# A fixed engine order for the row norms ahead of three projections, and the setup loads on ScalarE's queue

## The chip, the cores and the metric

The kernel runs on one core of a Trainium2 chip. The metric is the device time of one execution in microseconds (us). The engines are named as in the profile: PE (TensorE, matmuls and transposes), DVE (VectorE), ACT (ScalarE), POOL (GpSimd) and SP (SyncE, which here only issues DMAs). Each engine works through its own instructions in a fixed sequence and waits for the others by semaphores.

## The reference

The kernel computes one layer on 1024 rows of 1024 float32 numbers: a feed-forward half step, two attentions side by side, and a second feed-forward half step, each behind a row norm.

```python
def rms_norm(x, g):
    y = xf * lax.rsqrt(jnp.mean(xf * xf, axis=-1, keepdims=True) + EPS)
    return (y * g.astype(jnp.float32)).astype(x.dtype)

def swiglu_ffn(x, w_in, w_out):
    gate, up = jnp.split(x @ w_in, 2, axis=-1)
    return (jax.nn.silu(gate) * up) @ w_out
...
        x = x + 0.5 * swiglu_ffn(rms_norm(x, ffn1_norm[li]), ffn1_w_in[li], ffn1_w_out[li])
        u = rms_norm(x, mix_norm[li])
        proj = u @ w_mix_in[li]
...
        g_a, g_b = jnp.split(jax.nn.sigmoid(gate_logits + b_gate[li]), 2, axis=-1)
        merged = g_a * (y_a @ w_branch_a[li]) + g_b * (y_b @ w_branch_b[li])
        x = x + merged @ w_o[li]
        x = x + 0.5 * swiglu_ffn(rms_norm(x, ffn2_norm[li]), ffn2_w_in[li], ffn2_w_out[li])
    return rms_norm(x, final_norm)
```

The change touches the three norms ahead of `ffn1_w_in`, `w_mix_in` and `ffn2_w_in`, the first products of these three projections, and the loads of small tables (`lambda_*`, `subln_g`, `b_gate` and the two bias tables).

## The kernel before

**Products.** A projection is done block by block of 1024 x 1024 by 256 columns, called a pair: two column blocks `c1` and `c2` of 128 columns. Each pair is seven products instead of eight (`PRODUCTS`, line 158), in the manner of Strassen and Winograd. The operands of the activations are A11, A12, S1, S2, S3, S4 and A22, where S1 to S4 are sums and differences of the four quadrants; those of the weights are B11, B21, B22 and the differences T1, T2, T3 and N4. One product is twelve matmuls of 128x512: four steps over k, and for each three matmuls (`mm3`, line 126: high by high, high by low, low by high), since every operand is split into a rounded high part and a low rest. `split` (line 94) does that: ACT casts the high part (line 97), DVE subtracts it from the source (line 102). In the rows `whi` and `wlo` are the parts of a weight, `S1h` and `S1l` those of S1, and so on.

**The norm.** Rows 0 to 511 (four tiles of 128 rows, t = 0 to 3) are the first half, rows 512 to 1023 the second. For a tile, ACT squares and sums the row (line 174), DVE adds epsilon, POOL takes the power -1/2 (`r`, line 139), DVE multiplies row, `r` and gain. Then PE transposes the tile (line 208, eight transposes of 128x128), and ACT and DVE make the operands from it. The first half gives A11 and A12 (`norm0`). A tile of the second half gives, with the tile of the first half, S1 and in its place the source of S3 (`norm1a`), then S2 and S4 (`norm1b`), then S3 and A22 split (`norm1c`).

**Begun pairs.** Products 0 (A11 by B11) and 2 (A12 by B21) need the first half alone. So five pairs (`HEADS`, line 49; seven in the mixer) are begun with these two products (`Pair.head`, line 343) while the second half is normed. `Combine` (line 266) keeps the accumulation banks: one product is left in its bank for the chain that goes on in it, the other is copied out by ACT (`c`, line 287) and DVE adds the second product to that copy (`c<-prod,c`, line 113), called the take below. PSUM has six banks of tag "mm" for products and two of tag "tr" for transposes. After the second half is there, `Pair.rest` does the five remaining products of every pair; it loads both weight blocks (512 KB each, `raw`).

**Where it happens.** The norm ahead of the first feed-forward part stands at lines 657 to 689. Those ahead of the mixer and the second feed-forward part are the three callbacks of `renorm` (line 545); `late` (line 564) is their second half and runs when the last outputs of the projection before are out (`xc<-po`, line 522).

**What sets the order.** A scheduler orders the instructions on each engine; the code's order and the buffers limit it. Buffers rotate: ten slots `raw` (rows and weight blocks), ten `w` (split weights), ten `f` (temporaries of 256 KB), three `t` (weight differences). `setup` (line 601) loads the small tables on POOL's queue when the program begins; `le` (line 776) is the exponential of a `lambda` dot product on ACT.

Of the kernel before, what the change touches and what calls it, by code (L numbers as in the profile page):

```python
# [16 lines left out]
P = 128  # L17
# [37 lines left out]
def hybrid_layer_kernel(ctx, tc, x, ffn1_norm, ffn1_w_in, ffn1_w_out, mix_norm, w_mix_in,  # L55
# [165 lines left out]
    def norm1a(t, row0, row1, u, ps):  # L221

        a11, (a21, a22) = by_k(halves(row0.x)[0]), [by_k(h) for h in halves(row1.x)]
        t22 = turned(halves(row1.x)[1], ps)
        nc.scalar.copy(out=a22, in_=t22)
        t21 = turned(halves(row1.x)[0], ps)
        s1 = row1.s1 = temp([P, 4, P], "s1")
        add(s1, t21, a22)
        put(u, "S1", t, s1)
        add(a21, a11, t21, ALU.subtract)  # L230

    def norm1b(t, row0, row1, u):

        a11, a12 = (by_k(h) for h in halves(row0.x))
        add(a11, row1.s1, a11, ALU.subtract)
        put(u, "S2", t, a11)
        add(a12, a12, a11, ALU.subtract)
        put(u, "S4", t, a12)

    def norm1c(t, row1, u):  # L240

        for half, name in zip(halves(row1.x), ("S3", "A22")):
            put(u, name, t, by_k(half))
# [75 lines left out]
    class Pair:  # L319
# [23 lines left out]
        def head(self):  # L343
            r1 = self.load(0)
            get = weight_ops({"B11": r1[:, :4], "B21": r1[:, 4:]}, [P, 4, P])
            for m in (0, 2):
                self.product(m, get)
                self.todo.remove(m)
# [16 lines left out]
    def ffn_in(w_in, u, ps, extra=None):  # L365
# [48 lines left out]
        for p in pairs[:HEADS]:  # L414
            p.head()
            yield
# [128 lines left out]
    def renorm(x_dst, gain, u, ps, projection, extra_heads=0):  # L545
# [12 lines left out]
        def mid(rows):  # L558
            for t in range(4):
                row1.append(Row(rows[t]))  # L560
                nc.sync.dma_start(out=x_dst[4 + t][:, HALF:], in_=rows[t][:, HALF:])
                row1[t].take_right(gain)

        def late(rows):
            u.update(new_u(("S1", "S2", "S4")))
            for t in range(4):
                nc.sync.dma_start(out=x_dst[4 + t][:, :HALF], in_=rows[t][:, :HALF])
                row1[t].take(0)
                row1[t].scale_halves(gain)
                norm1a(t, row0[t], row1[t], u, ps)  # L570
            for _ in range(4 + extra_heads):
                next(projection, None)
            for t in range(4):
                norm1b(t, row0[t], row1[t], u)
            next(projection, None)
            u.update(new_u(("S3", "A22")))
            for t in range(4):
                norm1c(t, row1[t], u)
        return early, mid, late
# [21 lines left out]
    def setup(ps):  # L601
# [7 lines left out]

        for q, k in ((lambda_q1, lambda_k1), (lambda_q2, lambda_k2)):  # L610
            qk = []
            for v in (q, k):
                vt = small.tile([P, B_DIM], F32, tag="lv", bufs=2, name="lv")
                nc.gpsimd.dma_start(out=vt, in_=v[0].partition_broadcast(P))
                qk.append(vt)
            dot = small.tile([P, 1], F32, tag="dot", name="dot")
            nc.vector.tensor_tensor_reduce(out=qk[0], in0=qk[0], in1=qk[1], scale=1.0, scalar=0.0,
                                           op0=ALU.mult, op1=ALU.add, accum_out=dot)
# [19 lines left out]
        yield  # L638
        ea = stage([P, EA], "ea")
        n_clip = EA - (2 * REL_CLIP + 1)  # L640
        nc.gpsimd.dma_start(out=ea[:, n_clip:], in_=spread(rel_bias_a[0], A_HEADS, 2 * REL_CLIP + 1))
# [5 lines left out]
        nc.gpsimd.dma_start(out=tb, in_=spread(t5_bias, B_HEADS, 32))  # L647
# [9 lines left out]
    with tc.tile_pool(name="ps1", bufs=1, space=PSUM) as ps:  # L657

        u = new_u(U_OPS)
        ones = const.tile([1, P], F32, name="ones")  # L660
        nc.vector.memset(ones, 1.0)
        gain = sb.tile([P, D], F32, tag="gain", bufs=1, name="gain")
        for part in range(2):
            g_row = wtemp([1, HALF], "g_row")
            nc.scalar.dma_start(out=g_row, in_=ffn1_norm[0][part * HALF:(part + 1) * HALF].rearrange("(o d) -> o d", o=1))
            pg = ps.tile([P, HALF], F32, tag="mm", bufs=6, name="pg")
            nc.tensor.matmul(pg, ones, g_row, start=True, stop=True)
            nc.scalar.copy(out=halves(gain)[part], in_=pg)
        ffn1 = ffn_in(ffn1_w_in[0], u, ps, setup(ps))
        row0, row1 = [], []  # L670
        for t in range(4):
            row0.append(Row(load(rows(x)[t], raw_tile([P, D], "xt"))))
            row0[t].take()
            row0[t].scale(gain)
            norm0(t, row0[t], u, ps)
        next(ffn1, None)
        for t in range(4):
            row1.append(Row(load(rows(x)[4 + t], raw_tile([P, D], "xt"))))
            row1[t].take()
            row1[t].scale(gain)  # L680
            norm1a(t, row0[t], row1[t], u, ps)
        for _ in range(3):
            next(ffn1, None)
        for t in range(4):
            norm1b(t, row0[t], row1[t], u)
        next(ffn1, None)
        for t in range(4):
            norm1c(t, row1[t], u)
# [60 lines left out]
        def mixer_in():  # L749
# [5 lines left out]
            for p in pairs[8:15]:  # L755
                p.head()
                yield
# [8 lines left out]
        mix = mixer_in()  # L766
        out_projection(ffn1_w_out[0], stored, FFN_ORDER, FFN_LOADS, 0.5, rows(x), x_mid, ps,
                       *renorm(x_mid, gain, u2, ps, mix, 2))
# [237 lines left out]
    with tc.tile_pool(name="ps3", bufs=1, space=PSUM) as ps:  # L1006

        mo = {(th, g): big([P, 4, HALF], f"m{th}{g}", F32) for g in range(2) for th in range(2)}
        for jj in range(KT // 2):
            wr = load(w_cols(w_branch_b[0], jj * 256, 256, 0, 4), raw_tile([P, 4, 256]))  # L1010
            for odd in range(2):
                j = 2 * jj + odd
                w = split_units(wr[:, :, odd * P:(odd + 1) * P], branch_unit)
                for th in range(2):
# [4 lines left out]
                    for k in range(4):  # L1019
# [5 lines left out]
        ffn2 = ffn_in(ffn2_w_in[0], u3, ps)  # L1025
        out_projection(w_o[0], lambda n, i: mo[int(n[1]), i // 4][:, i % 4, :], WO_ORDER, WO_LOADS, 1.0, x_mid, x_mix, ps,
                       *renorm(x_mix, gain, u3, ps, ffn2))
# [59 lines left out]
```

## Time and profile before

| | us |
|---|---|
| median of 3 runs | 2115.09 (2113.3 to 2116.64) |
| the profiled execution | 2114.65 |
| its span in the trace | 2112.9 |
| PE busy | 2045.6 (97% of the span) |
| DVE busy, ACT busy | 1379.1 (65%), 955.5 (45%) |

In rows of the timeline the columns are: start in us, duration in us, engine, line, operation, output<-inputs, shape, count, and in brackets the idle time of the engine just before and what ended it. Rows of windows give the stretch, its length, then busy time and (number of instructions) of PE, the weight load, DVE, ACT and POOL, the granted clock of PE (1.00 is full), the DMA share and GB/s. Durations overlap on one engine: its instructions follow each other somewhat faster than they last.

### The profile page before, as it was taken

What the parts mean: (1) busy time and instruction counts of PE and PEld (TensorE: products, weight loads), DVE (VectorE), ACT (ScalarE), POOL (GpSimd) and SP (SyncE); (2) the same over time, 40 slices, a digit from 0 to 9 for tenths busy, and PEclk for the clock granted to TensorE, in tenths of its full rate; (3) what the DMA queues carried; (4) which work ended last, traced back from release to release, by engine and by line L of the source; (5) the groups of instructions that cost most, each with busy time, mean ns of one, the idle gap of its engine ahead of it and who ended that gap; (6) DMA issues with size and microseconds to landing.
All of it is one profiled execution on the core that took longest, in us unless ns stands there. A gap on an engine that the chain in (4) does not pass through costs nothing.

```text
span 2112.9 us, 28240 instructions
## 1 busy us (share of the span) xinstructions
PE 2045.6 (97%) x9901; PEld 1700.4 (80%) x9901; DVE 1379.1 (65%) x2459; ACT 955.5 (45%) x1825; POOL 142.8 (7%) x202
## 2 busy tenths in 40 slices
PE   6899999999999999999999999999899999999997
PEld 4688888888888788899877888787788888888886
DVE  6765656658567856654657787668766666668566
ACT  6433333334446644433467666157433333334444
POOL 2300000000001000000046211000000000000001
PEclk9999999999999999999999999999999999999999
DMA  5743323376344644743495365644542333275334
GB/s 166 213 135 100 125 86 104 105 261 214 99 135 143 195 135 130 234 145 115 158 302 178 111 221 167 229 139 127 163 144 91 125 96 107 92 278 201 99 116 160
DMA packets 272996, 324.61 MB, mean 154 GB/s; under 512 B 15070, under 2 KB 167662, under 8 KB 272852
## 3 DMA queue, kind: packets, MB, share of 16 engines
q1 hardware_dynamic: 271664, 319.55, 46.2%
q0 software_dynamic: 1184, 3.24, 0.6%
q8 instruction: 78, 1.28, 0.2%
q14 instruction: 66, 0.54, 0.1%
q10 hardware_dynamic: 4, 0.00, 0.0%
HBM read 221.74 MB, written 100.99 MB: 153 GB/s over the span
## 4 chain that ended last, share of the span: by engine, by line
PE 86%; DVE 6%; issue 3%; ACT 2%; DMA 2%; POOL 0%; SPq 0%; ACTq 0%; DVEq 0%; POOLq 0%
PE prod L128 19%; PE prod L129 19%; PE prod L130 18%; PE po L129 7%; PE po L128 7%; PE po L130 7%; PE pt L822 2%; DVE wlo L102 2%; PE pv L906 1%; PE pb L128 1%; PE pb L129 1%; PE pb L130 1%; PE sc L806 1%; PE sc L807 1%; PE pv L970 1%
## 5 line engine op out<-in xcount | busy, mean ns | idle before, releaser
L129 PE MATMUL po<-wlo,whi 128*128 128x512 f32 x744 | 291.1, 391 | 1.9 <-DVE wlo L102 1.8
L130 PE MATMUL po<-whi,wlo 128*128 128x512 f32 x744 | 289.6, 389 | 0.0
L97 ACT CAST whi<-raw 128x512 fp32r<-128x512 f32 x200 | 124.1, 622 | 294.3 <-PE prod L129 224.4
L97 ACT CAST whi<-T 128x512 fp32r<-128x512 f32 x192 | 119.1, 622 | 260.5 <-PE prod L129 248.0
L97 ACT CAST whi<-B 128x512 fp32r<-128x512 f32 x186 | 115.8, 622 | 262.1 <-PE po L129 255.0
L113 DVE TENSOR_TENSOR c<-prod,c 128x512 f32<-128x512 f32 x190 | 130.9, 690 | 146.1 <-PE prod L130 130.0
L102 DVE TENSOR_TENSOR wlo<-B,whi 128x512 fp32r<-128x512 f32 x186 | 128.1, 689 | 139.4 <-ACT whi L97 139.4
L102 DVE TENSOR_TENSOR wlo<-T,whi 128x512 fp32r<-128x512 f32 x192 | 131.8, 688 | 116.0 <-ACT whi L97 104.6
L128 PE MATMUL po<-whi 128*128 128x512 f32 x744 | 201.2, 390 | 0.0
L102 DVE TENSOR_TENSOR wlo<-raw,whi 128x512 fp32r<-128x512 f32 x200 | 137.3, 688 | 92.5 <-ACT whi L97 59.4
L129 PEld LDWEIGHTS po<-wlo,whi 128*128 128x128 f32 x744 | 139.6, 188 | 33.3 <-DVE wlo L102 4.6
L128 PEld LDWEIGHTS po<-whi 128*128 128x128 f32 x744 | 139.4, 188 | 29.0 <-ACT whi L97 0.2
L130 PEld LDWEIGHTS po<-whi,wlo 128*128 128x128 f32 x744 | 139.8, 188 | 28.4
L139 POOL TENSOR_TENSOR r<-v,neg_half 128x1 f32<-128x1 f32 x32 | 29.0, 913 | 1362.9 <-DVE v L180 1288.3
L102 DVE TENSOR_TENSOR wlo<-N,whi 128x512 fp32r<-128x512 f32 x64 | 44.1, 690 | 108.4 <-PE prod L129 69.0
L102 DVE TENSOR_TENSOR wlo<-ha,whi 128x512 fp32r<-128x512 f32 x154 | 105.5, 685 | 9.3 <-ACT whi L97 9.3
L287 ACT COPY c<-prod 128x512 f32<-128x512 f32 x186 | 102.1, 585 | 17.2 <-issue 10.5
L128 PE MATMUL prod<-A11h,whi 128*128 128x512 f32 x240 | 96.4, 402 | 7.9 <-DVE c L113 6.7
L816 ACT ACTIVATE pm<-pm,mn 128x640 f32<-128x640 f32 (+7 forms) x128 | 93.9, 735 | 19.7 <-DVE mn L814 17.0
L97 ACT CAST whi<-ha 128x512 fp32r<-128x512 f32 x154 | 94.8, 615 | 16.9 <-PE prod L129 11.4
L128 PE MATMUL prod<-A12h,whi 128*128 128x512 f32 x240 | 94.7, 394 | 3.4 <-DVE c L113 3.4
L814 DVE CUSTOM_DVE_ANT_0 pm<-sc,nb 128x640 f32<-128x640 f32 (+7 forms) x128 | 87.6, 701 | 14.7 <-PE sc L807 9.8
(236 smaller groups left out, 5018.8 us busy)
## 6 DMA issues: line engine op xcount, KB each, us to landing
raw<-in_ffn_w_in_dram SPq DMA_DIRECT2D x98, 512.0 KB, 4.2
raw<-in_w_mix_in_dram SPq DMA_DIRECT2D x47, 512.0 KB, 4.7
ha<-hS SPq DMA_DIRECT2D x88, 256.0 KB, 2.6
hA<-c SPq DMA_DIRECT2D x66, 256.0 KB, 4.1
ha<-hA SPq DMA_DIRECT2D x66, 256.0 KB, 2.7
B<-in_ffn_w_out_dram SPq DMA_DIRECT2D x12, 1024.0 KB, 11.7
hS<-hs SPq DMA_DIRECT2D x44, 256.0 KB, 2.4
hS<-c SPq DMA_DIRECT2D x44, 256.0 KB, 4.2
```

The lines of the kernel that those rows point to most:

```text
L97: nc.scalar.copy(out=hi, in_=src)
L102: (nc.gpsimd if on_pool else nc.vector).tensor_tensor(out=lo, in0=src, in1=h, op=ALU.subtract)
L113: nc.vector.tensor_tensor(out=out_, in0=a, in1=b, op=op)
L128: nc.tensor.matmul(ps, a[0], b[0], start=first, stop=False, skip_group_check=shared)
L129: nc.tensor.matmul(ps, a[0], b[1], start=False, stop=False, skip_group_check=shared)
L130: nc.tensor.matmul(ps, a[1], b[0], start=False, stop=last, skip_group_check=shared)
L139: nc.gpsimd.tensor_tensor(out=r, in0=v, in1=neg_half, op=ALU.pow)
L287: nc.scalar.copy(out=self.held[name], in_=p)
L806: nc.tensor.matmul(sc[:, m, :wc], qs[:, h, c], ks[:, h, kc], start=True, stop=False)
L814: nc.vector.tensor_tensor_reduce(out=d3, in0=sc, in1=nb.rearrange("p (n w) -> p n w", n=n), scale=1.0, scalar=3e38, op0=ALU.add, op1=ALU.m ...
L816: nc.scalar.activation(out=dst, in_=dst, func=AF.Exp, bias=mn, scale=-1.0, accum_out=rs)
L822: nc.tensor.transpose(pt[:, b, :], p, ident)
```

## The change

The first norm and the second halves in `renorm` are now written in a fixed order for each engine (`in_order`): ACT, DVE and PE in `renorm.late`, and POOL and SP too in the first norm. Within such a block the scheduler keeps the order of the code. `Pair.head` is cut into steps (`open` loads the weights, `hi` and `lo` split one, `multiply` does the matmuls, `taken` the copy or take), and `norm1a` to `norm1c` into the steps of `SecondHalf`. In the first norm the weights of four begun pairs are loaded as two blocks of 256 KB into slots `f` (`wraw`), left and right halves of a row are scaled apart, and DVE copies the gain. `setup` loads on ACT's queue, and in steps at pairs 5, 8, 11 and 14 rather than at the beginning.

```diff
+        def turn(self, t):
+            for n in (1, 0):
+                self.tr[t, n] = turned(halves(self.row1[t].x)[n], self.ps)
+        def keep(self, t):
+            nc.scalar.copy(out=by_k(halves(self.row1[t].x)[1]), in_=self.tr[t, 1])
+        def sums(self, t):
...
+            add(s1, self.tr[t, 0], a22)
+            add(a21, a11, self.tr[t, 0], ALU.subtract)
+        def first_hi(self, t):
+            nc.scalar.copy(out=self.part("S1", t)[0], in_=self.s1[t])
+        def first_lo(self, t):
...
+            add(l, self.s1[t], h.bitcast(F32), ALU.subtract)
+        def second(self, t):
+            a11 = by_k(halves(self.row0[t].x)[0])
+            add(a11, self.s1[t], a11, ALU.subtract)
+            put(self.u, "S2", t, a11)
...
+    def in_order(*engines):
+        return tc.manual_schedule(engines={getattr(mybir.EngineType, e) for e in engines})
...
+            with in_order("Activation", "DVE", "PE"):
+                heads[0].weights(0)
+                heads[0].weights(2)
+                heads[0].multiply(0)
+                heads[1].weights(0)
+                heads[0].multiply(2)
+                heads[0].taken(0)
+                heads[1].multiply(0)
+                for t in range(4):
+                    n, m = (t + 3) // 2, 2 - 2 * (t % 2)
+                    if t % 2 == 0 and n + 1 < len(heads):
+                        heads[n + 1].open()
+                    half.turn(t)
+                    half.keep(t)
+                    half.sums(t)
+                    half.first_hi(t)
+                    heads[n].weights(m)
+                    half.first_lo(t)
+                    if t < 3:
+                        heads[n].multiply(m)
+                    if t % 2 == 0:
+                        heads[n - 1].taken(2)
+                        heads[n].taken(0)
+                todo = [half.second] * 4 + [half.fourth] * 4
+                step = 0
+                for n in range(3, len(heads)):
+                    if n > 3:
+                        heads[n].weights(0)
+                    heads[n].multiply(0)
...
+                    heads[n].weights(2)
...
+                    for _ in range(2):
+                        if step < 8:
+                            todo[step](step % 4)
+                            step += 1
+                    heads[n].multiply(2)
...
-                nc.gpsimd.dma_start(out=vt, in_=v[0].partition_broadcast(P))
...
+                nc.scalar.dma_start(out=vt, in_=v[0].partition_broadcast(P))
...
+            p0.open(True)
+            p1.open(True)
...
+            half.turn(3)
+            p3.multiply(0)
+            half.keep(3)
+            half.sums(3)
+            half.first_hi(3)
+            p4.weights(0)
+            half.first_lo(3)
+            p2.taken(2)
+            p3.multiply(2)
+            p3.taken(0)
+            p4.weights(2)
+            half.second(0)
+            half.second(1)
+            p4.multiply(0)
+            p3.taken(2)
+            half.second(2)
```

ACT in the second half ahead of the second feed-forward part, before. `xc<-tr` is the copy of a transposed tile, `S1h<-s` the cast of S1, `whi<-raw` the cast of a begun pair's weight:

```order
L97 CAST whi<-raw 128x512
L197 ACTIVATE xc<-xc,r 128x512
L97 CAST whi<-raw 128x512
L225 COPY xc<-tr 128x512
L97 CAST S1h<-s_13783 128x4x128
L97 CAST S2h<-xt 128x4x128
L97 CAST whi<-raw 128x512
L97 CAST S4h<-xt 128x4x128
```

and in the changed kernel, at the same place, from the last scaled row on; `c` is the copy of a product, and line 447 its silu:

```order
L197 ACTIVATE xc<-xc,r 128x512 x3
L232 COPY xc<-tr 128x512
L244 CAST S1h<-s_13887 128x4x128
L375 CAST whi<-raw 128x512
L447 ACT_TABLE_LOAD
L447 ACTIVATE c_13859<-c_13859 128x512
L309 COPY c_13912<-prod 128x512
L232 COPY xc<-tr 128x512
L244 CAST S1h<-s_13925 128x4x128
L375 CAST whi<-raw 128x512
```

Before, two of these weights are cast ahead of the first copy; now the cast of each stands behind the copy and the S1h of its tile.

Further on in the same block, the changed kernel's ACT:

```order
L244 CAST S1h<-s_13998 128x4x128
L375 CAST whi<-raw 128x512
L447 ACTIVATE c_13985<-c_13985 128x512
L375 CAST whi<-raw 128x512
L97 CAST S2h<-xt 128x4x128 x2
L309 COPY c_14048<-prod 128x512
L97 CAST S2h<-xt 128x4x128 x2
L447 ACTIVATE c_14048<-c_14048 128x512
L375 CAST whi<-raw 128x512 x2
L97 CAST S4h<-xt 128x4x128 x2
```

The last begun pair's two weights (`x2`) stand behind all four casts of S2 and a silu. On PE the eight transposes of a tile stand between two products of twelve matmuls, and nothing else is there.

DVE in the first norm of the changed kernel, where the last begun pair's weight is split and the first pair that goes on gets its difference T1 (`T_727`, from a second load of the weights):

```order
L113 TENSOR_TENSOR wlo<-raw,whi 128x512
L113 TENSOR_TENSOR xt<-s_494,xt 128x512
L102 TENSOR_TENSOR S2l<-xt,S2h 128x4x128
L113 TENSOR_TENSOR xt<-s_538,xt 128x512
L113 TENSOR_TENSOR T_727<-raw 128x512
L102 TENSOR_TENSOR S2l<-xt,S2h 128x4x128
L113 TENSOR_TENSOR c_640<-prod,c_640 128x512
```

Before, the piece of DVE's order with the same difference (`T_716`) and the takes is:

```order
L102 TENSOR_TENSOR wlo<-raw,whi 128x512
L113 TENSOR_TENSOR T_716<-raw 128x512
L102 TENSOR_TENSOR A22l<-xt,A22h 128x4x128
L102 TENSOR_TENSOR S3l<-xt,S3h 128x4x128
L113 TENSOR_TENSOR xt<-xt 128x512
L102 TENSOR_TENSOR S2l<-xt,S2h 128x4x128
L113 TENSOR_TENSOR T_737<-raw,T_716 128x512
L113 TENSOR_TENSOR T_776<-raw 128x512
L113 TENSOR_TENSOR s_476<-tr,xt 128x512
```

In the changed kernel the four rows after `wlo` lead to T1 with S2 alone, and the take `c_640` stands two rows behind T1; before, sums of the third tile come next.

More of the change, by code (lines that the diff above doesn't have):

```diff
@@ L219, in norm0 @@
             nc.scalar.copy(out=by_k(half), in_=tr)
[L221 to L238, printed above, removed]
@@ L240, in norm1c, with __init__, part, fourth @@
-    def norm1c(t, row1, u):
-        for half, name in zip(halves(row1.x), ("S3", "A22")):
-            put(u, name, t, by_k(half))
+    class SecondHalf:
+        def __init__(self, row0, row1, u, ps):
+            self.row0, self.row1, self.u, self.ps, self.tr, self.s1 = row0, row1, u, ps, {}, {}
+        def turn(self, t):
[4 more added lines that the diff above has]
+        def sums(self, t):
+            a11, (a21, a22) = by_k(halves(self.row0[t].x)[0]), [by_k(h) for h in halves(self.row1[t].x)]
+            s1 = self.s1[t] = temp([P, 4, P], "s1")
+            add(s1, self.tr[t, 0], a22)
+            add(a21, a11, self.tr[t, 0], ALU.subtract)
+        def part(self, name, t):
+            return [v[:, :, t * P:(t + 1) * P] for v in self.u[name]]
+        def first_hi(self, t):
+            nc.scalar.copy(out=self.part("S1", t)[0], in_=self.s1[t])
+        def first_lo(self, t):
+            h, l = self.part("S1", t)
+            add(l, self.s1[t], h.bitcast(F32), ALU.subtract)
[3 more added lines that the diff above has]
+            put(self.u, "S2", t, a11)
+        def fourth(self, t):
+            a11, a12 = (by_k(h) for h in halves(self.row0[t].x))
+            add(a12, a12, a11, ALU.subtract)
+            put(self.u, "S4", t, a12)
+        def last(self, t):
+            for half, name in zip(halves(self.row1[t].x), ("S3", "A22")):
+                put(self.u, name, t, by_k(half))
@@ L341, in load, with open, hi, lo @@
             return load(w_cols(self.w, self.c[n], P), raw_tile([P, KT, P]))
[L343 to L348, printed above, removed]
+        def open(self, small=False):
+            if small:
+                self.raw = {m: load(w_cols(self.w, self.c[0], P, 2 * m, 4), temp([P, 4, P], "wraw")) for m in (0, 2)}
+            else:
+                r = self.load(0)
+                self.raw = {0: r[:, :4], 2: r[:, 4:]}
+            self.ops = {}
+        def hi(self, m):
+            self.ops[m] = [unit([P, 4, P], n) for n in ("whi", "wlo")]
+            nc.scalar.copy(out=self.ops[m][0], in_=self.raw[m])
+        def lo(self, m):
+            add(self.ops[m][1], self.raw[m], self.ops[m][0].bitcast(F32), ALU.subtract)
+        def weights(self, m):
+            self.hi(m)
+            self.lo(m)
+        def multiply(self, m, k0=0, k1=4):
+            acc, _ = self.sums.acc(m)
+            w, a = self.ops[m], self.u[PRODUCTS[m][0]]
+            for k in range(k0, k1):
+                mm3(acc, [v[:, k, :] for v in w], [v[:, k, :] for v in a], k == 0, k == 3)
+            self.acc = getattr(self, "acc", {})
+            self.acc[m] = acc
+        def taken(self, m):
+            self.sums.after(m, self.acc[m])
+            self.todo.remove(m)
         def rest(self):
@@ L413, in ffn_in @@
         pairs = [Pair(w_in, j * P, FF + j * P, u, ps, make_sink(j)) for j in range(NF)]
-        for p in pairs[:HEADS]:
-            p.head()
-            yield
+        opened += pairs[:HEADS]
+        yield
         for j, p in enumerate(pairs):
@@ L543, in stored, with renorm @@
         return load(h_ops[name][i], stored.tile[:, i % 4, :])
-    def renorm(x_dst, gain, u, ps, projection, extra_heads=0):
+    def renorm(x_dst, gain, u, ps, heads):
         row0, row1 = [], []
@@ L569, in late @@
                 row1[t].scale_halves(gain)
[L570 to L578, printed above, removed]
+            half = SecondHalf(row0, row1, u, ps)
+            for p in heads[:2]:
+                p.open()
@@ new lines, in late @@
+            with in_order("Activation", "DVE", "PE"):
[27 more added lines that the diff above has]
+                    heads[n].multiply(0)
+                    if n == 3:
+                        heads[2].taken(2)
+                    heads[n].weights(2)
+                    if n + 1 < len(heads):
+                        heads[n + 1].open()
+                    for _ in range(2):
[3 more added lines that the diff above has]
+                    heads[n].multiply(2)
+                    heads[n].taken(0)
+                    for _ in range(2):
+                        if step < 8:
+                            todo[step](step % 4)
+                            step += 1
+                    heads[n].taken(2)
+                while step < 8:
+                    todo[step](step % 4)
+                    step += 1
+                u.update(new_u(("S3", "A22")))
+                for t in range(4):
+                    half.last(t)
@@ L659, in hybrid_layer_kernel @@
         u = new_u(U_OPS)
[L660 to L681, printed above, removed]
@@ L764, in hybrid_layer_kernel @@
         gain = load_gain(mix_norm[0])
-        mix = mixer_in()
+        heads = []
+        mix = mixer_in(heads)
+        next(mix)
         out_projection(ffn1_w_out[0], stored, FFN_ORDER, FFN_LOADS, 0.5, rows(x), x_mid, ps,
-                       *renorm(x_mid, gain, u2, ps, mix, 2))
+                       *renorm(x_mid, gain, u2, ps, heads))
         run_all(mix)
@@ L1024, in hybrid_layer_kernel @@
         u3 = {}
-        ffn2 = ffn_in(ffn2_w_in[0], u3, ps)
+        heads = []
+        ffn2 = ffn_in(ffn2_w_in[0], u3, ps, heads)
+        next(ffn2)
         out_projection(w_o[0], lambda n, i: mo[int(n[1]), i // 4][:, i % 4, :], WO_ORDER, WO_LOADS, 1.0, x_mid, x_mix, ps,
-                       *renorm(x_mix, gain, u3, ps, ffn2))
+                       *renorm(x_mix, gain, u3, ps, heads))
         run_all(ffn2)
```

169 lines of the change are left out of this document (147 added, 22 removed).

## The prediction

> **What bounds the kernel now.** I read the page's busy times first, then the windows of an undisturbed stretch and of the three norms, then PE's timeline there.
>
> ```profile
> span 2112.9 us, 28240 instructions
> PE 2045.6 (97%) x9901; PEld 1700.4 (80%) x9901; DVE 1379.1 (65%) x2459; ACT 955.5 (45%) x1825; POOL 142.8 (7%) x202
> ```
> ```profile
> 150.00:400.00 250.00, 250.00 (x1105) 207.06 (x1104) 150.33 (x233) 90.74 (x157) 0.00 (x0) 1.00 0.32 101
> ...
> 0.00:30.00 30.00, 11.29 (x32) 6.26 (x32) 17.81 (x35) 19.80 (x38) 13.98 (x22) 1.00 0.71 215
> 700.00:710.00 10.00, 7.97 (x31) 6.16 (x31) 10.00 (x18) 7.99 (x17) 0.00 (x0) 0.83 0.54 152
> 1470.00:1480.00 10.00, 4.86 (x28) 3.65 (x26) 10.00 (x18) 8.80 (x17) 0.00 (x0) 0.92 0.71 207
> 1480.00:1490.00 10.00, 6.64 (x18) 5.28 (x19) 10.00 (x18) 6.23 (x11) 0.00 (x0) 0.56 0.38 111
> ```
>
> PE bounds nearly everything: 2112.9 − 2045.6 = 67 us idle in all, and in 150 to 400 us none. There a matmul takes 250/1105 = 0.226 us, a product of twelve 2.72. PE waits in the norms, where DVE is full (10.00 of 10). So a new order can win only there.
>
> ```profile
> 30.61 0.79 PE L128 MATMUL prod<-A11h,whi 128*128 128x512 f32 x1 [0.67 <-ACT A11h L97]
> 61.48 0.79 PE L128 MATMUL prod<-A12h,whi 128*128 128x512 f32 x1 [3.37 <-DVE c L113]
> 90.95 0.39 PE L128 MATMUL prod<-A22h,whi 128*128 128x512 f32 x1
> 680.36 1.88 DVE L522 SCALAR_TENSOR_TENSOR xc<-po,xc 128x512 f32<-128x512 f32 x3
> 700.63 0.66 PE L208 MATMUL tr<-ident,xc 128*128 128x128 f32 x4 [0.55 <-ACT xc L225]
> 702.29 0.66 PE L208 MATMUL tr<-ident,xc 128*128 128x128 f32 x4 [1.00 <-ACT xc L225]
> 703.42 0.63 PE L128 MATMUL prod<-A11h,whi 128*128 128x512 f32 x1 [0.48 <-ACT p L287]
> 745.09 0.39 PE L128 MATMUL prod<-A22h,whi 128*128 128x512 f32 x1
> 1453.67 2.48 DVE L522 SCALAR_TENSOR_TENSOR xc<-po,xc 128x512 f32<-128x512 f32 x4
> 1476.00 0.66 PE L208 MATMUL tr<-ident,xc 128*128 128x128 f32 x4 [1.56 <-ACT xc L225]
> 1483.36 0.79 PE L128 MATMUL prod<-A11h,whi 128*128 128x512 f32 x1 [6.70 <-DVE c L113]
> 1500.52 0.50 PE L128 MATMUL prod<-S1h,whi 128*128 128x512 f32 x1 [0.78 <-DVE c L113]
> 1504.02 0.50 PE L128 MATMUL prod<-S2h,whi 128*128 128x512 f32 x1 [0.48 <-ACT whi L97]
> 1515.09 0.39 PE L128 MATMUL prod<-A22h,whi 128*128 128x512 f32 x1
> ```
>
> I measure each norm by one pair of marks: from the program's start, or from the first last output (`xc<-po`), to the first product with A22, when all operands are there. These are 90.95 us, 745.09 − 680.36 = 64.7 in the mixer, and 1515.09 − 1453.67 = 61.4 ahead of the second feed-forward part. The last loses 1.56 + 6.70 + 0.78 + 0.48 = 9.5 to waits; the 6.70 is a bank whose take stood in DVE's queue behind norm work. After it the clock falls to 0.56: some twelve matmuls of 0.43 instead of 0.23, 2.4 us more. Clean it is 61.4 − 11.9 = 49.5. The mixer loses 0.55 + 1.00 + 0.48 before 703.42 and I put the same 0.78 + 0.48 later, 3.3 in all, and about 1.7 by clock (0.83 in its window): clean 59.7. Those are what a perfect order could win: 12 and 5 us. In the first norm products begin at 30.61; 192 product matmuls (43.5) and the transposes stand before 90.95, so some 40 us are lost.
>
> **The two second halves, in `renorm.late`.** What counts is that PE, ACT and DVE each follow the code. PE has the eight transposes of tile t, then one product, then the next transposes, and nothing to put between. That product's weight is cast on ACT behind the copy and behind S1h, and S1h waits for DVE's sum. The links are all in the trace of before, where products filled them:
>
> ```profile
> 1462.54 1.04 PE L208 MATMUL tr<-ident,xc 128*128 128x128 f32 x8
> 1463.33 0.69 DVE L102 TENSOR_TENSOR wlo<-raw,whi 128x512 fp32r<-128x512 f32 x1 [0.46 <-ACT whi L97]
> 1463.34 0.47 PE L128 MATMUL prod<-A12h,whi 128*128 128x512 f32 x1
> 1464.34 0.57 ACT L225 COPY xc<-tr 128x512 f32<-128x512 f32 x1
> 1465.07 0.68 DVE L113 TENSOR_TENSOR s<-tr,xc 128x512 f32<-128x512 f32 x1
> 1465.79 0.62 ACT L97 CAST S1h<-s 128x512 fp32r<-128x512 f32 x1 [0.88 <-DVE s L113]
> 1466.38 0.69 DVE L113 TENSOR_TENSOR xt<-s,xt 128x512 f32<-128x512 f32 x1
> 1467.11 0.62 ACT L97 CAST S2h<-xt 128x512 fp32r<-128x512 f32 x1 [0.70 <-DVE xt L113]
> ```
> ```profile
> 12.74 1.14 ACT L97 CAST whi<-raw 128x512 fp32r<-128x512 f32 x2 [0.28 <-DMA raw<-in_ffn_w_in_dram]
> ```
>
> A round from its first transpose: 0.60 for four transposes (half of the eight, with their tail), 0.57 for the copy, 0.68 for the sum, 1.14 for two casts in a row (S1h and the weight), and four hand-overs of 0.04 (the sum ends at 1465.75, S1h begins at 1465.79): 3.15 us until the product begins. Its third matmul waits for `wlo`, 0.73 after the cast, with two matmuls (0.45) before: 0.28 more. So a round lasts 3.15 + 2.72 + 0.28 = 6.15, against 0.80 (1462.54 to 1463.34) + 2.72 = 3.52 now. That is 2.63 lost, **10.5 for four rounds**.
>
> Then four tiles of S2 run as a relay: difference to S2h 0.73 (1466.38 to 1467.11), cast and hand-over 0.66, S2l a step of 0.60: 1.99 a tile, 8.0 for four. Behind them ACT has a silu that waits for a take, and only then the next begun pair's weight: 0.60 + 8.0 + 0.7 (take) + 0.55 + 0.62 = 10.4 from the beginning of the last `wlo`; PE has 0.73 + 10 matmuls (2.27) of this covered. **7.4 lost**. In the mixer two pairs more follow: the sixth's weights stand behind the four S4 tiles, the same 10.4 against two products (5.4), so **5** lost, and the seventh waits about 2 for its cast. Ahead of the second feed-forward part the S4 tiles come after the last begun product, and the differences T1 and T2 of the first pair share DVE and ACT with them: the same relay of 8.0 against two products, 3 to 5 more with the load that T1 waits for; I take 5.
>
> Warm sums: 49.5 + 10.5 + 7.4 + 5 = 72.4, against 61.4: **+11**. Mixer: 59.7 + 10.5 + 7.4 + 5 + 2 = 84.6, against 64.7: **+20**. What the new gaps do to the clock is bounded by nothing below and 1.7 per gap above, since gaps of 0.55, 1.00 and 0.48 at 700 to 703 were already followed by matmuls of 0.63 (a start every 0.43). With some six gaps in a stage that is 0 to 10; I take 3 each, as idle and work alternate and half of a cold spell lies within a wait. **+14 and +23.**
>
> The Trainium skill ("TensorE: Matmul & The Clock Gate", The HAM clock gate) has the array at half clock only after an idle window of about 3.4 us; by that, gaps of 2.6 would cost nothing. The rows at 700 to 703 speak against it. It is a rival below.
>
> **The first norm.**
>
> ```profile
> 1.53 1.28 ACT L174 ACT_TABLE_LOAD   x1 [1.53 <-PEq L1073]
> 4.47 1.06 ACT L174 ACTIVATE junk<-xt 128x1024 bf16<-128x1024 f32 x1 [1.65 <-DMA xt<-in_x_dram]
> 5.88 1.06 ACT L174 ACTIVATE junk<-xt 128x1024 bf16<-128x1024 f32 x1 [0.26 <-DMA xt<-in_x_dram]
> 9.44 0.22 DVE L617 CUSTOM_DVE_ANT_0 lv<-lv 128x64 f32<-128x64 f32 x1 [3.63 <-DMA lv<-in_lambda_k_dram]
> 9.71 0.20 ACT L776 ACTIVATE le<-dot 128x1 f32<-128x1 f32 x1 [2.21 <-DVE dot L617]
> 20.08 0.14 DVE L180 TENSOR_SCALAR v<-rsq 128x1 f32<-128x1 f32 x1
> 20.60 1.28 DVE L181 SCALAR_TENSOR_TENSOR xt<-xt,r,gain 128x1024 f32<-128x1024 f32 x1 [0.38 <-POOL r L139]
> 23.71 1.11 PE L208 MATMUL tr<-ident,xt 128*128 128x128 f32 x4 [1.68 <-ACT xt L219]
> ```
> ```profile
> raw<-in_ffn_w_in_dram SPq DMA_DIRECT2D x23, 512.0 KB, 4.7
> ```
>
> `le` held ACT for 2.21 us and goes; A11 of the four tiles comes before everything else. Rows land 1.4 us apart at first (4.47, 5.88), 2.4 at the 215 GB/s of the first window, so the fourth at 9 to 10; I take 9.5. Its square with the read-out lasts 1.25, v to the scaling 0.52, half a row's scaling some 0.7, four transposes 1.11, the cast 0.62: the first product begins at about 14 and not 30.61, a lead of 17. Then it is spent. PE waits about 1.2 for A12's low part, 2 at the third turn, 3.9 at the fourth (the eighth row's square stands on ACT behind a silu). The second load of the first pair's weights needs the raw slot of the last begun pair, so it starts when that pair's `wlo` is done, near 52; T1 stands three steps behind that `wlo` on DVE and waits 4.7 for the load (median in the first 120 us), and the take behind T1 frees the bank that PE's next product needs: 6 lost. The S4 tiles behind the next T1 cost 6.7 in the same way. With 1.8 of cold clock after both and some 5 of cold beginning and short waits, that is 28, and A22 comes at 14 + 47 (work left) + 28 = 89 to 90: **−1**. It is −17 if the loads are in before T1 asks, +5 if they take the 8.9 that `x` took.
>
> ```profile
> xt<-in_x_dram SPq DMA_DIRECT2D x8, 512.0 KB, 8.9
> ```
>
> **Setup on ACT's queue.** Two table loads more (1.28 each) on an ACT that is busy 45%, and a transpose on PE that waits for a load: nothing where weights are several products ahead, 3 where not. I take **+1**. Gain copies by DVE and the smaller weight loads are in the walk.
>
> Sum: −1 + 23 + 14 + 1 = **+37** on the profiled 2114.65, 2151.7; the median is 0.4 above that run, which changes nothing: **2151**.
>
> **The rivals.**
> - *The first norm keeps its lead.* The loads land in time, the takes are free: −17 instead of −1, **2135**. For it: the begun weights are smaller blocks. Against it: T1's load cannot start before a slot is free. Still slower than before.
> - *The clock stays full in the short gaps*: 6 less, **2145**, inside the main case.
> - *Faster: the rounds are covered.* If the weight casts ran ahead of S1h, as the change's cut into steps could let them, a round would stay at 3.52 and 8 × 2.63 = 21 and the clock's 6 go. With the first norm's lead kept as well, +37 − 27 − 16 = −6, **2109**; if also the S2 relay is covered in both places (15), 2094. It decides from a round of about 4.4 us on: below that, with the lead kept, the change wins. Against it stand the order's rows: each cast of these weights is behind S1h.
> - *Setup stalls PE*, or cold clock on every gap: up to 14 more, **2165**.
>
> **How the numbers follow.** Main case (with the clock's rival), 2138 to 2165: 0.62. Lead kept, 2125 to 2138: 0.17. Rounds covered: 0.16, of which 0.12 below 2110 and 0.04 near no change. Above 2165: 0.05. A measurement of this kernel can tell about 0.2% (4 us) from no change. Faster 0.12, same 0.04, slower 0.84. The range leaves out most of the fast case and the last: 2112 to 2165.
>
> **What would show it.** In the profile after, the first product near 14 and the first A22 near 90; in both second halves rounds of transposes and one product about 6 us apart, with `whi` ending PE's wait; a wait of over 7 us ahead of the fifth begun pair's products (about 5 ahead of the sixth's in the mixer); windows with a clock under 1.00 there; A22 some 75 and 88 us behind `xc<-po`. Rounds of 3.5 us, or the first A22 near 74, would prove me wrong.

## The result, and the profile after

The changed kernel takes 2167.56 us (median of 4 runs, 2166.56 to 2169.32) against 2115.28 before: a ratio of 1.0249, 95% interval 1.0231 to 1.0267. It is slower, as forecast, but by 52 us where the sum gave 37, and 2.6 us outside the range.

The page of the changed kernel: PE is busy 20.7 us longer with the same 9901 instructions, and idle 2167.2 − 2066.3 = 101 us instead of 67.

```profile
span 2167.2 us, 28226 instructions
PE 2066.3 (95%) x9901; PEld 1709.0 (79%) x9901; DVE 1380.9 (64%) x2464; ACT 959.2 (44%) x1825; POOL 129.2 (6%) x194
```

The changed kernel's timeline at the marks of the prediction, PE and DVE:

```profile
13.85 0.79 PE L128 MATMUL prod<-A11h,whi 128*128 128x512 f32 x1 [0.68 <-ACT A11h L782]
59.68 0.77 PE L128 MATMUL prod<-A12h,whi 128*128 128x512 f32 x1 [5.43 <-DVE c L113]
76.41 0.79 PE L128 MATMUL prod<-S4h,whi 128*128 128x512 f32 x1 [5.29 <-ACT S4h L97]
89.73 0.39 PE L128 MATMUL prod<-A22h,whi 128*128 128x512 f32 x1
...
687.28 2.47 DVE L567 SCALAR_TENSOR_TENSOR xc<-po,xc 128x512 f32<-128x512 f32 x4
781.14 0.39 PE L128 MATMUL prod<-A22h,whi 128*128 128x512 f32 x1
1492.49 2.48 DVE L567 SCALAR_TENSOR_TENSOR xc<-po,xc 128x512 f32<-128x512 f32 x4
1569.34 0.39 PE L128 MATMUL prod<-A22h,whi 128*128 128x512 f32 x1
```

Cut at these marks, the two spans compare like this (us):

| stretch | before | after | difference | forecast |
|---|---|---|---|---|
| start to the first A22 (first norm) | 90.95 | 89.73 | −1.2 | −1 |
| to the mixer's `xc<-po` (setup lies here) | 589.41 | 597.55 | +8.1 | +1 |
| to the mixer's first A22 | 64.73 | 93.86 | +29.1 | +23 |
| to the last part's `xc<-po` (attention) | 708.58 | 711.35 | +2.8 | 0 |
| to its first A22 | 61.42 | 76.85 | +15.4 | +14 |
| to the end | 597.81 | 597.86 | 0 | 0 |
| sum | 2112.9 | 2167.2 | +54.3 | +37 |

**The second halves.** The first round in the mixer, PE, ACT and DVE, and PE's waits that follow:

```profile
695.97 1.03 PE L208 MATMUL tr<-ident,xc 128*128 128x128 f32 x8
696.66 0.59 ACT L232 COPY xc<-tr 128x512 f32<-128x512 f32 x1 [2.54 <-PE tr L208]
697.28 0.69 DVE L113 TENSOR_TENSOR s<-tr,xc 128x512 f32<-128x512 f32 x1 [3.00 <-ACT xc L232]
698.00 0.62 ACT L244 CAST S1h<-s 128x512 fp32r<-128x512 f32 x1 [0.76 <-DVE s L113]
698.53 0.61 ACT L375 CAST whi<-raw 128x512 fp32r<-128x512 f32 x1
699.19 0.50 PE L128 MATMUL prod<-A12h,whi 128*128 128x512 f32 x1 [2.19 <-ACT whi L375]
705.55 0.50 PE L128 MATMUL prod<-A11h,whi 128*128 128x512 f32 x1 [2.19 <-ACT whi L375]
711.91 0.67 PE L128 MATMUL prod<-A12h,whi 128*128 128x512 f32 x1 [2.19 <-ACT whi L375]
719.58 0.50 PE L128 MATMUL prod<-A11h,whi 128*128 128x512 f32 x1 [2.19 <-ACT whi L375]
733.27 0.80 PE L128 MATMUL prod<-A11h,whi 128*128 128x512 f32 x1 [7.18 <-ACT whi L375]
746.84 0.79 PE L128 MATMUL prod<-A11h,whi 128*128 128x512 f32 x1 [4.96 <-ACT whi L375]
757.59 0.50 PE L128 MATMUL prod<-A11h,whi 128*128 128x512 f32 x1 [2.10 <-ACT whi L375]
```

The chain is the one that was added up: transposes, copy, sum, S1h, weight, product, 695.97 to 699.19 = 3.22 us (forecast 3.15). Every round's wait ends with `whi` after the same 2.19 us; from 699.19 to 705.55 a round lasts 6.36 (forecast 6.15). The three long waits are 7.18, 4.96 and 2.10, against 7.4, 5 and 2. ACT in the relay of S2 tiles ahead of the last part:

```profile
1529.32 0.62 ACT L97 CAST S2h<-xt 128x512 fp32r<-128x512 f32 x1 [1.36 <-DVE xt L113]
1531.29 0.62 ACT L97 CAST S2h<-xt 128x512 fp32r<-128x512 f32 x1 [1.36 <-DVE xt L113]
...
1537.22 0.63 ACT L447 ACTIVATE c<-c 128x512 f32<-128x512 f32 x1 [1.36 <-DVE c L113]
1537.76 1.12 ACT L375 CAST whi<-raw 128x512 fp32r<-128x512 f32 x2
```

A tile takes 1.97 us. ACT waits 1.36 us of it for DVE's difference, and DVE's next step waits 0.69 us for ACT's cast; the silu and the weights come at the end.

**The clock.** Windows of the changed kernel, with the granted clock as the number behind POOL's:

```profile
687.00:781.00 94.00, 69.69 (x276) 53.08 (x275) 53.79 (x88) 43.59 (x77) 2.51 (x4) 0.89 0.48 145
...
730.00:740.00 10.00, 6.73 (x17) 5.25 (x18) 5.84 (x10) 4.71 (x8) 0.00 (x0) 0.53 0.45 134
```

Over the mixer's stage the clock is 0.89: 0.11 x 94 = 10 us of full clock not granted, part of it within waits. Seventeen matmuls keep PE busy for 6.73 us in 730 to 740.

**Setup.** Between the first A22 and the mixer the time goes at one place. The changed kernel there, ACT with its queue (ACTq, DMA issues) and PE:

```profile
138.66 0.60 ACT L447 ACTIVATE gate<-prod 128x512 f32<-128x512 f32 x1 [10.26 <-PE prod L130]
138.67 0.37 ACTq L704 DMA_DIRECT2D lv<-in_lambda_q_dram  x1
139.08 0.44 ACTq L704 DMA_DIRECT2D lv<-in_lambda_k_dram  x1
139.56 0.44 ACTq L704 DMA_DIRECT2D lv<-in_lambda_q_dram  x1
140.04 0.44 ACTq L704 DMA_DIRECT2D lv<-in_lambda_k_dram  x1
140.58 0.59 ACT L309 COPY c<-prod 128x512 f32<-128x512 f32 x1 [1.31 <-DMA lv<-in_lambda_q_dram]
141.22 0.50 PE L128 MATMUL prod<-S3h,whi 128*128 128x512 f32 x1 [2.36 <-ACT c L309]
142.58 1.28 ACT L998 ACT_TABLE_LOAD   x1
147.44 0.50 PE L128 MATMUL prod<-S1h,whi 128*128 128x512 f32 x1 [1.46 <-ACT whi L97]
```

ACT sits idle for 10.26 us at a silu that waits for PE, and the loads are issued behind that silu. So no cast got ahead of it. The kernel before casts three weights ahead of the same silu:

```profile
131.73 0.62 ACT L97 CAST whi<-N 128x512 fp32r<-128x512 f32 x1 [2.10 <-PE prod L129]
134.45 0.62 ACT L97 CAST whi<-T 128x512 fp32r<-128x512 f32 x1 [2.10 <-PE prod L129]
137.17 0.62 ACT L97 CAST whi<-raw 128x512 fp32r<-128x512 f32 x1 [2.10 <-PE prod L129]
139.89 0.60 ACT L401 ACTIVATE gate<-prod 128x512 f32<-128x512 f32 x1 [2.10 <-PE prod L130]
```

In the changed kernel, when the silu is done, four issues of 0.4 us stand ahead of the copy that PE waits for, then two more issues, a table load and the exponentials ahead of the next weights. The cast behind PE's second wait has itself waited 1.23 us for DVE, which had stood 1.43 us for the loads to land. Windows there, of the changed kernel and then of the one before:

```profile
130.00:150.00 20.00, 16.09 (x60) 12.01 (x59) 9.93 (x22) 6.26 (x11) 0.24 (x1) 0.89 0.34 113
150.00:170.00 20.00, 20.00 (x84) 16.36 (x84) 13.38 (x22) 8.00 (x13) 0.00 (x0) 0.94 0.32 93
```
```profile
130.00:150.00 20.00, 20.00 (x90) 16.58 (x89) 13.86 (x23) 6.45 (x11) 0.00 (x0) 1.00 0.42 134
150.00:170.00 20.00, 20.00 (x90) 16.58 (x89) 10.68 (x17) 7.07 (x13) 0.00 (x0) 1.00 0.25 78
```

144 matmuls instead of 180 in the same 40 us: 36 x 0.226 = 8.1 us, all of the stretch's loss. Waits are 3.8 of it; most of the rest is the clock (0.89, 0.94).

### The profile page after: what moved, and what is told of

Its sections match the earlier page's. It is cut to its first block, busy times and chain, and to the rows that moved or that the text cites. A ratio compares the mean times of both kernels' runs of the same rounds, so it can differ in the third digit from the quotient of the medians.

```text
span 2167.2 us, 28226 instructions
## 1 busy us (share of the span) xinstructions
PE 2066.3 (95%) x9901; PEld 1709.0 (79%) x9901; DVE 1380.9 (64%) x2464; ACT 959.2 (44%) x1825; POOL 129.2 (6%) x194
## 3 DMA queue, kind: packets, MB, share of 16 engines
q8 instruction: 78, 1.28, 0.3%
## 5 line engine op out<-in xcount | busy, mean ns | idle before, releaser
L97 ACT CAST whi<-raw 128x512 fp32r<-128x512 f32 x166 | 103.4, 623 | 277.6 <-PE prod L129 229.4
L102 DVE TENSOR_TENSOR wlo<-raw,whi 128x512 fp32r<-128x512 f32 x166 | 114.3, 689 | 112.5 <-ACT whi L97 56.2
L128 PE MATMUL prod<-S4h,whi 128*128 128x512 f32 x240 | 94.2, 392 | 6.6 <-ACT S4h L97 5.3
L130 PE MATMUL prod<-A11h,wlo 128*128 128x512 f32 x240 | 97.3, 405 | 0.0
```

Source lines behind the costliest of these rows:

```text
L97: nc.scalar.copy(out=hi, in_=src)
L102: (nc.gpsimd if on_pool else nc.vector).tensor_tensor(out=lo, in0=src, in1=h, op=ALU.subtract)
L128: nc.tensor.matmul(ps, a[0], b[0], start=first, stop=False, skip_group_check=shared)
L130: nc.tensor.matmul(ps, a[1], b[0], start=False, stop=last, skip_group_check=shared)
```

## The experiments

Each run is cut at the same marks, read in its own timeline (us, with the span of the profiled execution and the median of all its runs):

| run | first norm | to mixer | mixer | attention | last part | to end | span | median |
|---|---|---|---|---|---|---|---|---|
| before | 90.95 | 589.41 | 64.73 | 708.58 | 61.42 | 597.81 | 2112.9 | 2115.3 |
| changed | 89.73 | 597.55 | 93.86 | 711.35 | 76.85 | 597.86 | 2167.2 | 2167.6 |
| 1 old second halves | 88.85 | 597.55 | 63.38 | 712.44 | 60.63 | 597.95 | 2120.8 | 2126.3 |
| 2 setup on POOL | 94.92 | 589.80 | 94.34 | 709.82 | 78.59 | 597.73 | 2165.2 | 2168.1 |
| 3 casts first | 90.18 | 597.54 | 87.04 | 712.03 | 70.37 | 597.84 | 2155.0 | 2155.5 |
| 4 casts and relay | 89.04 | 597.46 | 80.57 | 710.79 | 68.89 | 597.85 | 2144.6 | 2146.7 |
| 5 setup early | 92.65 | 593.71 | 94.14 | 708.81 | 77.04 | 597.95 | 2164.3 | 2166.6 |
| 6 fifth pair small | 87.19 | 595.74 | 95.96 | 709.74 | 78.47 | 598.50 | 2165.6 | 2172.4 |
| 7 parts together | 93.30 | 592.12 | 65.87 | 711.93 | 61.24 | 598.34 | 2122.8 | 2122.6 |
| 8 only second halves | 90.54 | 589.42 | 95.28 | 709.38 | 80.12 | 597.66 | 2162.4 | 2163.5 |
| 9 setup on SP | 95.57 | 589.79 | 94.14 | 709.37 | 80.04 | 597.59 | 2166.5 | 2169.5 |
| 10 short block | 81.00 | 597.63 | 94.09 | 708.47 | 78.29 | 597.92 | 2157.4 | 2162.2 |
| 11 combined | 82.04 | 589.82 | 64.68 | 708.66 | 61.20 | 598.20 | 2104.6 | 2110.3 |
| 12 combined, small | 81.81 | 590.04 | 65.58 | 711.03 | 61.41 | 598.43 | 2108.3 | 2110.5 |

**Runs 1 and 8: the second halves alone, taken out and put in.** Run 1 puts the order of before back:

```diff
-            half = SecondHalf(row0, row1, u, ps)
...
+            for t in range(4):
+                norm1a(t, row0[t], row1[t], u, ps)
+            for p in heads[:-1]:
+                p.head()
+            for t in range(4):
+                norm1b(t, row0[t], row1[t], u)
+            heads[-1].head()
```

> The changed kernel with the second halves ahead of the mixer and of the second feed-forward part as they were before (scheduler's order); first norm and setup stay changed. Theory (the second halves cost 29.1 + 15.5 = 44.6 us between their marks, and it all goes when they go): about 2123 us, marks at 64.7 and 61.4 us again. Rival (the fixed order of the first norm or the setup loads delay later stages too, so that the losses are shared): over 2135 us, with the marks back but time lost elsewhere.

Measured 2126.34 us, ratio to before 1.0047 (1.0031 to 1.0064). Run 8 is the kernel before with only `renorm` replaced:

> The kernel before with nothing changed but the fixed order of the two second halves. Theory (the parts add up): 2115.3 + 29.1 + 15.5 = 2160 us. Rival (the second halves cost so much only behind the changed first norm and setup): under 2150 us.

Measured 2163.54, ratio 1.0222 (1.0208 to 1.0236). The stages go where the theory has them: 63.38 and 60.63 without the fixed order, 95.28 and 80.12 with it, whatever stands ahead. The fixed order of the second halves costs 41 to 48 us, so most of the result. The rest of the change costs 11 us by run 1 and 4 by run 8. Seven of the profiles have the same code in the last part's norm, and it takes 76.85 to 80.12 us in them.

**Run 3: the cast ahead of the transposes.**

```diff
+                    heads[n].weights(m)
                     half.turn(t)
                     half.keep(t)
                     half.sums(t)
                     half.first_hi(t)
-                    heads[n].weights(m)
                     half.first_lo(t)
```

> The changed kernel with one step moved in the rounds of the second halves: the begun pair's weight is cast and split ahead of the tile's transposes, no longer behind S1h. Theory (the cast behind S1h sets the round): rounds of 3.5 us instead of 6.36, 8 x 2.84 = 23 us less, and some clock with it: 2138 to 2145 us. Rival (the transposes' two banks or DVE set the round): rounds stay over 5 us and the time over 2155.

Measured 2155.52 us, ratio 1.0181 (1.0165 to 1.0196): 12 us less than the changed kernel, half of what the theory wanted, and the time that the rival named. PE and ACT in the mixer of run 3:

```profile
696.41 1.04 PE L208 MATMUL tr<-ident,xc 128*128 128x128 f32 x8
700.04 1.03 PE L208 MATMUL tr<-ident,xc 128*128 128x128 f32 x8
...
701.05 0.56 ACT L309 COPY p<-prod 128x512 f32<-128x512 f32 x1
701.52 0.62 ACT L375 CAST whi<-raw 128x512 fp32r<-128x512 f32 x1
702.19 0.50 PE L128 MATMUL prod<-A11h,whi 128*128 128x512 f32 x1 [1.12 <-ACT whi L375]
705.33 1.03 PE L208 MATMUL tr<-ident,xc 128*128 128x128 f32 x8
...
726.18 0.80 PE L128 MATMUL prod<-A11h,whi 128*128 128x512 f32 x1 [7.21 <-ACT whi L375]
```

The first round is 3.63 us, as it should be, and its wait of 2.19 is gone: S1h ahead of the cast was what set the round. The second and the fourth still wait 1.12 (the second lasts 5.29), because there an activation that waits for a take, and a copy, stand ahead of the cast; and the relay's 7.21 is untouched. The chain was right, but it was one of two that ACT's order held.

**Run 4: the relay too.** Beside the edit of run 3, the next begun pair's weights are split ahead of two tiles, and their loads are opened earlier:

```diff
-                    if n > 3:
-                        heads[n].weights(0)
                     heads[n].multiply(0)
...
                     if n + 1 < len(heads):
-                        heads[n + 1].open()
+                        heads[n + 1].weights(0)
                     for _ in range(2):
...
                     heads[n].taken(0)
+                    if n + 1 < len(heads):
+                        heads[n + 1].weights(2)
+                    if n + 2 < len(heads):
+                        heads[n + 2].open()
```

> As the run with the casts first, and also the weights of the next begun pair are split ahead of two tiles of S2 or S4 instead of behind four. Theory (the relay of S2 tiles ahead of the weights costs 7.2 + 5.0 + 2.1 in the mixer and 7.1 ahead of the second feed-forward part): 21 us less than the run with the casts first, 2118 to 2125 us. Rival (PE only waits later, at the first products with S2 and S4, which need the relay's end anyway): half of it comes back, over 2130 us.

Measured 2146.72 us, ratio 1.0143 (1.0128 to 1.0158): 9 less than run 3, so the rival was the nearer one. PE in run 4:

```profile
726.59 0.50 PE L128 MATMUL prod<-A11h,whi 128*128 128x512 f32 x1 [3.26 <-ACT whi L375]
740.51 0.79 PE L128 MATMUL prod<-A11h,whi 128*128 128x512 f32 x1 [5.67 <-ACT whi L375]
```

Two tiles ahead of a weight instead of four leave 3.26 of run 3's 7.21, and 1.67 comes back one product later. The wait after that is 5.67, against 6.57 in run 3 and 4.96 in the changed kernel: there an activation stands ahead of the weight and has waited 3.77 us for DVE. What stands ahead of a weight on ACT, PE pays here. The scheduler's order, which put weights between all of these, needs 63 to 66 us for the stage in runs 1, 7, 11 and 12, against 80.57 here.

**Runs 2, 5 and 9: where setup's loads stand.** The edit in run 2 is this, and the same with `nc.sync` in run 9:

```diff
-                nc.scalar.dma_start(out=vt, in_=v[0].partition_broadcast(P))
+                nc.gpsimd.dma_start(out=vt, in_=v[0].partition_broadcast(P))
```

> The changed kernel with the table loads of setup on POOL's queue again, at the same places in the program. Theory (six loads issued from ACT's queue, 0.4 to 0.5 us each, stand ahead of the copies and casts that PE waits for near 140 us): 7 to 8 us less, about 2160 us, and no wait of PE over 0.5 us between 100 and 200 us. Rival (the table of the exponential and the late place of setup cost it, whichever queue loads): within 3 us of 2167.6.

> The changed kernel with setup's loads on SP's queue, where they stand behind the first norm's own loads; no engine that computes issues them, and none stands ahead of a copy or cast. Theory (place and queue cost 7.8 us): from the first A22 to the mixer's mark 589 to 591 us, the first A22 within 2 us of 89.7, about 2160 us. Rival (the dot products wait on DVE for loads that are not in yet, inside the first norm): the first A22 at 92 us or later, 2164 us or more.

In run 5 five of the loads stay on ACT, at the program's start:

```diff
             nc.scalar.dma_start(out=g_row, in_=ffn1_norm[0].rearrange("(n d) -> n d", n=2))
+            next(tables)
```

> The changed kernel with five of setup's six loads still on ACT's queue but issued at the program's start, behind the gain's load and ahead of the first square, where ACT waits for rows anyway. Theory (it is the place, in front of casts that PE is about to need, and not the queue, that cost 7.8 us between the first A22 and the mixer): from the first A22 to the mixer's mark 590 us again, the first norm within 1 us, about 2160 us. Rival (ACT's queue costs wherever it issues): first products later by 2 to 3 us, and 2163 to 2168 us.

Measured 2168.09, 2169.46 and 2166.57 us (ratios 1.0243, 1.0246 and 1.0245, all within 0.0016): by the total none of the moves matters, and by the total alone the theory would be dead. The marks show effects that cancel. Off ACT's queue the stretch to the mixer is 589.8 in both runs, 7.8 us less and within 0.4 of before: that much setup on ACT at its late place did cost. ACT casts its three weights ahead of the silu again there, with 2.10 us of idle time before it. It isn't the issues alone that went, because the scheduler then put the `lambda` loads, their dot products and the exponentials into the first norm, and the first A22 is 5.2 and 5.8 us later. The last part's norm, 1.7 and 3.2 us longer, takes more of the gain; its code is the same. POOL and DVE in run 2, then PE in run 9:

```profile
3.16 0.33 POOL masks.py:199 TENSOR_SCALAR_AFFINE_SELECT ident<-ident 128x128 f32<-128x128 f32 x1
63.91 0.69 DVE L113 TENSOR_TENSOR T<-raw 128x512 f32<-128x512 f32 x1 [5.57 <-DMA raw<-in_ffn_w_in_dram]
```
```profile
65.50 0.76 PE L128 MATMUL prod<-A12h,whi 128*128 128x512 f32 x1 [7.46 <-DVE c L113]
```

In run 2 POOL's issues stand ahead of the identity matrix that the first matmuls need (3.16 instead of 1.02), and T1 waits 5.57 us for its load, where the changed kernel's T1 waits 1.79; in run 9 T1 waits 6.10. Run 5 is in between: 593.7, since one load and its transpose stay at the late place, and 92.65. ACT's idle time of 10.26 us at the silu is still there, with that single issue of 0.34 us behind it, and PE waits 1.43 us for the load. So half of the 8.1 us goes with the five loads, the dot products and the exponentials, and half stays with one load behind the silu on ACT. In runs 2 and 9 POOL and SP issue this load near 124 us, and its transpose at 133 to 134 costs PE no more than 0.4. Place and queue together make the cost.

**Runs 6 and 10: the first norm.** Run 6 loads the fifth pair in two blocks (`p4.open(True)`), run 10 ends the fixed order early:

```diff
             p4.weights(2)
-            half.second(0)
-            half.second(1)
-            p4.multiply(0)
...
+        p4.multiply(0)
+        p3.taken(2)
+        p4.taken(0)
+        p4.multiply(2)
+        p4.taken(2)
+        for t in range(4):
+            half.second(t)
+            half.fourth(t)
```

> The changed kernel with the fifth begun pair's weights in the first norm loaded as two blocks of 256 KB into slots f too, so that the second load of the first pair's weights finds a free raw slot. Theory (T1 on DVE waits for that load, and PE's 5.4 us wait for a take behind it comes from there): that wait goes, the first A22 at 83 to 85 us, about 2161 us. Rival (the ten f slots become the bound: a sum waits for the store that empties its slot): the wait turns into another before a turn, A22 stays at 88 to 91, 2166 to 2169 us.

> The changed kernel with the fixed order of the first norm ended when the last begun pair's weights are split; S2, S4, S3, A22 and the last begun products go to the scheduler. Theory (the relays of S2 and S4 tiles in their fixed order, with the takes and T1 among them, cost PE's waits of 5.4 and 5.3 us): the first A22 at 78 to 84 us, 2157 to 2162 us. Rival (DVE's work is the bound there in any order): A22 at 88 us or later, 2166 to 2169 us.

Run 6 gave 2172.43 us, ratio 1.0265 (1.0251 to 1.0279): no gain, although in its profiled execution A22 comes at 87.19 and the take's wait is halved to 2.56. Another of 3.67 us, for a weight ahead of S2, follows. Neither theory nor rival fits, and the run doesn't settle what the load alone is worth. Run 10 gave 2162.24, ratio 1.0212 (1.0198 to 1.0226), and A22 at 81.00, 8.7 us earlier in the profiled execution; the median gains 5.3. PE in run 10:

```profile
48.10 2.28 PE L208 MATMUL tr<-ident,xt 128*128 128x128 f32 x8 [5.37 <-DVE xt L765]
58.32 0.47 PE L128 MATMUL prod<-A11h,whi 128*128 128x512 f32 x1 [1.64 <-DVE c L113]
```

The waits of 5.43 and 5.29 at 59.68 and 76.41 are gone, down to 1.64 and less, though the fourth turn now waits 5.37 instead of 3.05. So it was the fixed order of the relays, with T1 and the takes between them, that spent about half of the lead of 17, and DVE's work is not the bound there.

**Runs 7, 11 and 12: the parts together.** Run 7 joins runs 1, 5 and 6; run 11 joins runs 1, 9 and 10; run 12 adds the fifth pair's blocks.

> The first norm in its new order with the fifth pair's weights in f slots, five of setup's loads at the start, and the second halves ahead of the mixer and of the second feed-forward part in the scheduler's order. If all three theories hold and the parts add up: 2126.3 - 7.8 - 5 = about 2113 us, at best 2108. If the setup's place or the f slots give their gain back: 2118 to 2126 us.

> The first norm's new order up to the last begun pair's weights, setup's loads on SP's queue, and the second halves of the mixer and of the second feed-forward part in the scheduler's order. If the parts add up: 2126.3 - 7.8 and what the shorter block gives (0 to 10): 2108 to 2118 us, so at best faster than before by 0.3%.

> As the combined kernel, and the fifth begun pair's weights in f slots, so that the next loads of whole blocks start earlier. Theory (T1's load is still late in the combined kernel): 2 to 5 us less than it. Rival (f slots bind, or T1 now stands on DVE ahead of a load that is not in): the same or more.

Run 7: 2122.57 us, ratio 1.0032 (1.0019 to 1.0045); its first norm pays with 93.30 for what setup saves. Run 11: 2110.26, **ratio 0.9964 (0.9951 to 0.9977)**: little, but clear of the interval, and less time than both kernels. Run 12 is the same, 0.9964 (0.9951 to 0.9978), so the fifth pair's blocks give nothing there, as its rival had it. In run 11 the first norm keeps 8.9 us of its lead, setup costs 0.4, and the second halves are those of before. Behind the short block setup's loads on SP cost the first norm only 1.0 us (82.04 against run 10's 81.00), not the 5.8 of run 9.

## Why the prediction came out as it did

The trace shows +54.3 where the sum gave +37. Of these 17 us, 7.1 came in the stretch of setup, 6.1 in the mixer's second half, 2.8 in attention and 1.4 in the last part's norm.

- *The second halves.* The mechanism was right. Run 3 shows the cast behind S1h in the round, run 4 the relay ahead of the weights, and runs 1 and 8 that this order makes nearly all of the result. The mixer's waits sum to 4 x 2.19 + 7.18 + 4.96 + 2.10 + 1.31 (at the first S4 product) = 24.3 us, and the terms 10.5 + 7.4 + 5 + 2 made 24.9.
- *The clock in them was mis-sized.* "I take 3 each" is the term: the mixer's 93.86 less the clean 59.7 and its waits of 24.3 leaves 9.9 for cold matmuls and waits too small to list. After the waits of 7.18 and 4.96 a product runs at 0.43 us a start (733.87, 734.29, 734.72 in the trace), and I had counted half a cold spell. In the whole stage 33 matmuls start 0.40 to 0.46 us after the one before instead of 0.226, which is 6.6 us; what is left, 3.3, is short waits and an inexact 59.7. In the last part 24 such matmuls cost 4.8, not 3, and the S4 tiles less than their term (1.28 + 1.57 + 1.04 = 3.9 instead of 5). That its +15.4 met +14 is partly luck: errors of both signs.
- *The step that failed is setup on ACT's queue*: "nothing where weights are several products ahead, 3 where not. I take +1". It was 8.1. I counted what the loads and the table cost ACT and took the usual lead of its casts as cover. But the loads stood behind a silu that waits for PE, and the casts that give the lead stood behind them, so the lead was used up before the first load was issued. Runs 2 and 9 show 7.8 by taking setup's loads off ACT, where ACT keeps its lead; run 5 shows that one late load on ACT is enough for half of it.
- *The first norm* came out at −1.2 with its waits where they were put: first product at 13.85 (14), 5.43 at the take (6), 5.29 at the S4 tiles (6.7). The reason given for the first holds only in part: T1 waits 1.79 us for its load, not 4.7, so the size came out right by some luck. Run 10 shows which order spent the lead.
- *Attention's 2.8 us* were not forecast and stay open. The stretch lies between 708.5 and 712.4 in all runs, without a rule that I could see; no run was made for it.
- *The rivals.* The lead of the first norm wasn't kept, the rounds weren't covered. The last rival, that setup stalls PE or cold clock follows every gap, came nearest: setup did stall PE, and the time lies 2.6 us above its 2165. Of the eight gaps of 2.19 us in the rounds, two were followed by a slow product (0.67 at 711.91, and 0.80 at 1510.96 in the last part); six were not. Over the seven profiles with this order (the changed kernel and runs 2, 5, 6, 8, 9 and 10) it was 27 of 56, so the same code loses a different amount each time. The Trainium skill ("TensorE: Matmul & The Clock Gate", The HAM clock gate) has the array cold after an idle window of about 3.4 us. The gaps without a slow product, run 3's gaps of 1.12, run 4's 3.26 and the long waits agree with it; the 27 and the rows at 700 to 703 of before speak against it as a bound on the gap. One rival was not tried: that transposes don't count as work. Eight of them (1.03 us) stand ahead of each such gap, so PE does no product for 3.22 us, and for 4.4 in the rows of before. Against it, the 4.8 us without a product at 41.0 to 45.8 in the changed kernel were followed by full clock. What decides stays open.

## What to carry to other kernels

When an engine's order is written by hand, look at each row that another engine waits for and ask what stands ahead of it that waits in turn: a copy, a sum and a cast in a row make one chain, and PE pays its full length unless something else is queued on PE. A DMA issued from an engine that computes takes a place in that engine's order, and can cost it the lead that it had. When two runs have the same total, cut them at marks before you say that an edit did nothing.

## What the runs showed of the hardware

In the second halves every wait of 5 to 7 us was followed by a cold spell, 5 to 13 matmuls some 0.43 us apart instead of 0.226. A gap of 2.19 us behind eight transposes was followed by one in two of eight in the changed kernel, and in 27 of 56 over the seven profiles with this order. Four DMA issues on ACT's queue took 0.37 to 0.44 us each, and ACT's next copy began only behind them.
